# Transposes of the last attention step in the scores' banks, first gate_up weights split by halves, early splits issued behind the exponentials

## The chip, the core and the metric

The kernel runs on one core of a Trainium2 chip. The core has five engines with a queue each: TensorE (PE, matmuls and transposes; its weight loads are listed as PEld), VectorE (DVE), ScalarE (ACT), GpSimd (POOL) and SyncE (SP), which here only issues DMAs. The metric is the device time of one execution in microseconds. Before the change the median of 3 runs is 1319.53 us (1319.31 to 1319.69).

## The reference

One encoder block on x of 1024 rows by 1024 columns, in float32: a norm, a token mixer of a gated short convolution and an attention with 8 heads of 64, a merge of the two branches, an output projection, a second norm, a SwiGLU layer with 2816 hidden columns, and residual sums.

```python
h = rmsnorm(x, norm_mix_pre)
m = mixer(h, w_in, b_f, conv_w, w_branch, w_out)
x = x + rmsnorm(m, norm_mix_post)
h = rmsnorm(x, norm_ffn_pre)
f = swiglu(h, w_gate_up, w_down)
x = x + rmsnorm(f, norm_ffn_post)

# in the mixer
logits = q @ k.T * scale + c[q_pos] - c[k_pos]      # causal, per head
yb = softmax(logits) @ v
merged = sigmoid(gate_conv) * (ya @ w_branch[0]) + sigmoid(gate_attn) * (yb @ w_branch[1])
m = merged @ w_out
```

## The kernel before

**Products.** Each float32 operand is split into two parts of a shorter type: `split(hi, lo, src)` copies on ACT (`hi`) and subtracts on DVE (`lo = src - hi`), and a product of 128x128 by 128x512 is three matmuls. `lo` therefore always waits for `hi`. The large products (w_in, w_out, gate_up, down) are Strassen products of half-size blocks.

**Attention.** The heads are taken in pairs (j = 0 to 3) with the queries in blocks of 128 rows. A list `steps` of 24 steps says which blocks stand in a step: (7), (6), (5), (4), (3, 2), (1, 0) for the first three pairs. In step t of the loop at L1284 stand, in this order of the code: the scores of step t (`step_qk`, PE, into banks `sp` of the tag "S", two tiles of two banks each); the transposes of the probabilities of step t-1 (`turn_bank`, PE, into banks `tps` of the tag "T", two of them), each drained to `ptT` by ACT or DVE; the row maxima of step t (`row_max`: on DVE, `pt` and `nm`, which frees the score tile), and the exponentials (`expo`: on ACT, `pt`). The product with v (`pv_pair`, banks `po`) follows some steps behind. For a step with one block, the maxima and exponentials of head e = 0 come in the first half of the step (`now[0]`), those of e = 1 in the second (`now[1]`).

Between them `fills()` issues what is listed for the step: the ACT half of splits of later operands (`cuts`), whose DVE halves are collected in `lows` and issued at the end of the step, and from step 7 on twelve matmuls at a time of the convolution's branch product (`branch_a`, bank `pba`, closed by a DVE product into `um`). In steps 2 to 5 the splits are those of k and q of the second head pair (`hi<-lo`, `hi<-raw`), in step 6 those of two tiles of the convolution's output (`yh`, `yl`) and of one weight (`s4h`, `s4l`).

In this stage every engine keeps the order of the code (`strict[0] = engines`, L1107): an instruction that waits holds all that stands behind it on its engine.

After the last step (t = 24, `NU`) the ten transposes of step 23 remain, two `turn_bank` for each head, then the reciprocal of the row sums (`inverse(3)`, DVE), its transpose `tr` on PE (`inverse_rows`, in t = 25), and two small DMAs by way of DRAM that spread it over rows (`rb`), by which `yb` is divided before the second branch product (`pbb`).

**gate_up.** Its first four weights (`begin_early`, `f_begin`, `prep_first`) are begun while the w_out products and the second norm of the last row pairs still run (`e_norm`, `e_turn`). A weight is loaded into one of three buffers `raw` (512 KB), split, and its first half `LO` multiplied (A11), its second half `UP` later (A12). The same three buffers hold rows of the norm. Outside the attention a scheduler sets the order on each engine from the order of the code and from what it takes for each instruction's time, apart from calls that are `pinned`.

Of the kernel before, what the change touches and what calls it, by code (L numbers as in the profile page):

```python
# [10 lines left out]
F32 = mybir.dt.float32  # L11
# [6 lines left out]
P = 128  # L18
S = 1024
# [3 lines left out]
NC = 512  # L23
# [23 lines left out]
def block_kernel(  # L47
# [17 lines left out]
    engines = ("tensor", "vector", "scalar", "gpsimd", "sync")  # L65
# [28 lines left out]
    def pool(name, bufs=1, side="left", space=None):  # L94
        kw = dict(name=name, bufs=bufs)
        if space is not DRAM:
            kw["reuse_waits"] = "tile"
        if space is not None:
            kw["space"] = space
        else:  # L100
            kw["side"] = side
        stack = ExitStack()
        ctx.callback(stack.close)
        return stack.enter_context(tc.tile_pool(**kw)), stack.close

    def f32(ap):
        return ap.bitcast(F32)
# [4 lines left out]
    def sub(o, a, b):  # L112
        nc.vector.tensor_tensor(o, a, b, op=ALU.subtract)
# [14 lines left out]
    def copy(o, a):  # L128
        nc.scalar.activation(o, a, AF.Copy)

    def split(hi, lo, src):

        copy(hi, src)
        sub(lo, src, f32(hi))
# [9 lines left out]
    cpool, _ = pool("const")  # L144
    stat, _ = pool("stat", 4, side="right")
    stat.tile([P, 56], F32, name="pad", bufs=1)
    dpool, _ = pool("dram", space=DRAM)
# [383 lines left out]
    wpool, _ = pool("w")  # L531
# [4 lines left out]
    def kblk(t):  # L536
        return t.rearrange("p (a b) -> p a b", b=P)
# [4 lines left out]
    def raw_t():  # L542
        return wtile("raw", 3)

    def hi_t():
        return wtile("hi", 4, F32R)

    def lo_t():
        return wtile("lo", 3, F32R)
# [10 lines left out]
    def kmaj(src):  # L560
        return src.rearrange("(k p) m -> p k m", p=P)

    LO, UP = slice(0, 4), slice(4, 8)

    def prep_first(src1, there=None):

        if there is None:
            r1 = raw_t()
            nc.sync.dma_start(r1, kmaj(src1))
            h1, l1 = hi_t(), lo_t()  # L570
            split(h1, l1, r1)
        else:
            r1, h1, l1 = there
        return dict(A11=(h1[:, LO], l1[:, LO]), A12=(h1[:, UP], l1[:, UP])), r1
# [113 lines left out]
    def wcols(c0):  # L688
        return win[:, c0 : c0 + P]
# [147 lines left out]
    def p_cols(t, i, e):  # L837

        o = sum(x + 1 for x in steps[t][1] if x > i) * P
        return p_tile(t, e)[:, o : o + (i + 1) * P]  # L840
# [21 lines left out]
    def expo(t, i, e):  # L862

        c = e * ST + i
        pt = p_cols(t, i, e)
        nc.scalar.activation(
            pt, pt, AF.Exp, bias=nms.pop((t, i, e)), scale=-1.0,
            accum_out=rsums[steps[t][0]][:, c : c + 1],
        )

    def turn_bank(t, e, half, engine):

        n = sum(i + 1 for i in steps[t][1])
        ks = range(4 * half, min(4 * half + 4, n))
        if not ks:
            return
        if (t, e) not in ptTs:
            ptTs[t, e] = (
                t1.tile([P, ST, P], F32, tag="pT", name="ptT", bufs=6)
                if t  # L880
                else raw_t()
            )
        tps = pss.tile([P, 4, P], F32, tag="T", name="tps", bufs=2)
        for k in ks:
            nc.tensor.transpose(
                tps[:, k - ks[0], :], ps_[t, e][:, k * P : (k + 1) * P], ident
            )
        o, a = ptTs[t, e][:, ks[0] : ks[-1] + 1, :], tps[:, : len(ks), :]

        def drain():  # L890
            if engine == "ACT":
                copy(o, a)
            else:
                nc.vector.tensor_copy(o, a)

        return drain
# [3 lines left out]
    NU = len(steps)  # L900
# [95 lines left out]
    for ij, (kind, j, _, _) in enumerate(jobs):  # L996
# [10 lines left out]
        if ij < 2:  # L1007
            if ij == 0:
                r1 = raw_t()
                nc.sync.dma_start(r1, kmaj(wcols(jobs[1][2])))  # L1010
                t0_.tile([P, S], F32, tag="p", name="room", bufs=2)
                h1, l1 = (
                    kblk(t0_.tile([P, S], F32R, tag="cb", name=n, bufs=2)) for n in ("h1", "l1")
                )
# [8 lines left out]
            w = {**w, **prep_rest(wcols(jobs[ij][3]), r1)}  # L1023
            if ij == 1:
                pairs.q.append(pairs.prep(*pairs.srcs.popleft()))
            _, c12, c21, c22 = strassen(w, h1b, psm, pp, p1, mid)
# [7 lines left out]
        else:  # L1034
            w = pairs.get()
            psm_close()
            strict[0] = engines
            pss, pss_close = pool("pss", space=PSUM)
# [11 lines left out]
        elif kind == "gb":  # L1050
            for m, parts in ((j, (c11, c12)), (j + 1, (c21, c22))):
                zt = zts.pop(m)
                for n in range(2):
# [5 lines left out]
                    for t in (1, 0):  # L1059
                        back = 2 - t  # L1060
# [108 lines left out]
    def inverse(j):  # L1169

        invs[j] = st_tile("ri", 2 * ST)
        nc.vector.reciprocal(invs[j], rsums[j])

    def inverse_rows(j, psp, tag, bufs=1):

        tr = psp.tile([P, 4, P], F32, tag=tag, name="tr", bufs=bufs)[: 2 * ST, 0, :]
        nc.tensor.transpose(tr, invs[j], ident)

        def drain():
            rT = t0_.tile([H * ST, P], F32, tag="cT", name="rT")[: 2 * ST]  # L1180
            nc.vector.tensor_copy(rT, tr)
            for e in range(2):
                nc.sync.dma_start(
                    ri_dram[j][e].rearrange("(i p) -> i p", p=P), rT[e * ST : (e + 1) * ST, :]
                )
            rb = rbs[j] = tp_.tile([P, S], F32, tag="rb", name="rb", bufs=1)
            for e in range(2):
                nc.sync.dma_start(
                    rb[e * HD : (e + 1) * HD, :], ri_dram[j][e].partition_broadcast(HD)
                )  # L1190

        return drain
# [58 lines left out]
    cuts, at = defaultdict(list), defaultdict(list)  # L1251
# [32 lines left out]
    for t in range(2, NU + 2):  # L1284
        turned = None
        now = groups(t) if t < NU else ([], [])
        back = t - 1 if t <= NU else None
        wide = back and sum(i + 1 for i in steps[back][1]) > 6
        if t < NU:
            step_qk(t)  # L1290
        if t > 6:
            for u in due(t):
                pv_pair(u)
        if t in rows:
            turned = inverse_rows(rows[t], pst, "mb")
        if t == NU + 1:
            turned = inverse_rows(3, pss, "T", 2)
        lows, muls = [], []

        def fills():  # L1300
            lows.extend(f for f in (g() for g in cuts.pop(t, ())) if f)
            muls.extend(m for m in (next(fill, None) for _ in range(units.get(t, 0))) if m)

        if t == NU:
            fills()
        if back:
            da = turn_bank(back, 0, 0, "ACT")
            db = turn_bank(back, 0, 1, "DVE")
            da()
        if t <= 6:  # L1310
            for u in due(t):
                pv_pair(u)
        for i, e in now[0]:
            row_max(t, i, e)
        if t < NU and len(steps[t][1]) > 1:
            mask_of(t, steps[t][1][1])
        if turned:
            turned()
        if t == NU:
            for f in lows + muls:  # L1320
                f()
            lows, muls = [], []
        if back and db:
            db()
        for i, e in now[0]:
            expo(t, i, e)
        if t == NU:
            inverse(3)
        else:
            fills()  # L1330
        if back:
            dc = turn_bank(back, 1, 0, "ACT" if wide else "DVE")
            dd = turn_bank(back, 1, 1, "DVE" if wide else "ACT")
        for i, e in now[1]:
            row_max(t, i, e)
        if 7 < t < NU:
            for m in muls:
                m()
            muls.clear()
        if t == NU - 1:  # L1340
            for i, e in now[1]:
                expo(t, i, e)
        if back:
            dc()
            if dd:
                dd()
        if t < NU - 1:
            for i, e in now[1]:
                expo(t, i, e)
        if t + 1 < NU:  # L1350
            mask_of(t + 1, steps[t + 1][1][0])
        for f in lows + muls + at.pop(t, []):
            f()
# [152 lines left out]
    turned = []  # L1506
# [112 lines left out]
    for k in (0, 2):  # L1619
        w = ep.tile([P, D], F32, tag="t", name="wr", bufs=1)  # L1620
        cut_wo(w, ((B22, 4 + k, n2), (B22, 5 + k, n2)))

    def f_src(f):
        return wgu[:, f * P : (f + 1) * P], wgu[:, FH + f * P : FH + (f + 1) * P]
# [3 lines left out]

    def f_begin(n, b1, p1):
        f = FIRSTS[n]  # L1630
        w, _ = prep_first(f_src(f)[0])
        prod(b1, w["A11"], hb[B11], True)
        pinned(lambda: copy(p1, b1), *(("scalar",) if n >= 8 else ()))
        if f > 1:
            nc.gpsimd.dma_start(pre_dram[f][0], p1)
        begun[n] = w, b1, p1
# [90 lines left out]
    for n in range(4, NPRE + 1):  # L1727
# [6 lines left out]
        if n == 8:  # L1734
            for sl in range(4):
                a = slice(sl * P, (sl + 1) * P)
                b = slice(NC + sl * P, NC + (sl + 1) * P)
# [28 lines left out]
    for f in range(NF):  # L1766
        if f < NPRE:
# [7 lines left out]
            _, g2, u1_, u2 = strassen(rest.get(False), hb, psm, fp, p1, rest.more)  # L1775
# [275 lines left out]
```

## Time and profile before

| | us |
|---|---|
| median of 3 runs | 1319.53 |
| the profiled execution | 1319.29 |
| its span, from the first to the last instruction | 1317.2 |
| DVE busy in the span | 964.9 |
| ACT busy in the span | 556.8 |
| PE idle in the span (1317.2 - 1306.7) | 10.5 |

A row of a timeline gives the start in us from the span's start, the duration, the engine, the line (all have L76, that of the helper that records each call), the operation, what it writes and reads, the shape, and in brackets how long the engine was idle before it and what ended the wait. A row of waits gives who waited for whom: us in total, how often, the longest. PE's granted clock is 0.998 of full speed over the span.

A duration reaches past the point at which the next instruction can start: two ACT copies of 128x512, 0.6 us each by themselves, start 0.52 us apart.

### The profile page before, as it was taken

The page shows a single profiled execution, that of the slowest core. Times are in us where ns is not written, and L with a number is a line of the kernel's source. Part 1 is how long each engine was busy: PE and PEld are TensorE (multiplying, and loading weights), DVE is VectorE, ACT ScalarE, POOL GpSimd, SP SyncE. Part 2 cuts the span into 40 slices and gives each one's busy share as a digit, 9 for nine tenths or more (in the row PEclk, how much of TensorE's full clock was granted, in tenths as well). Part 3 has the DMA queues.
Part 4 walks back from the last instruction along what each step waited for, and adds up shares of the span by engine and source line. Part 5 has one row for each costly group of instructions (what it writes and reads, how often), then busy time and mean ns, then how long its engine had stood idle before and what let it go on. Part 6 is the DMA issues. An engine that isn't in the chain of part 4 may idle for free.

```text
span 1317.2 us, 17978 instructions
## 1 busy us (share of the span) xinstructions
PE 1306.7 (99%) x6710; PEld 1089.5 (83%) x6710; DVE 964.9 (73%) x1514; ACT 556.8 (42%) x895; POOL 142.4 (11%) x271
## 2 busy tenths in 40 slices
PE   9999999999999999999999999999999999999998
PEld 8988888888888888888888888888888888888886
DVE  6974878765656876686798788987766776676685
ACT  6642322243355866514577522322322234444452
POOL 0001000011012212020011021221001110000000
PEclk9999999999999999999999999999999999999999
DMA  6344544555536545465266455553223338866441
GB/s 217 113 120 136 150 123 121 153 164 146 152 120 200 161 144 171 152 232 208 76 228 207 153 168 177 176 184 104 97 88 118 106 111 282 317 249 193 158 168 64
DMA packets 189351, 211.00 MB, mean 160 GB/s; under 512 B 11584, under 2 KB 137600, under 8 KB 189264
## 3 DMA queue, kind: packets, MB, share of 16 engines
q1 hardware_dynamic: 155872, 146.64, 35.6%
q0 software_dynamic: 16496, 54.83, 11.2%
q10 hardware_dynamic: 16896, 8.39, 2.1%
q8 instruction: 52, 0.85, 0.3%
q14 instruction: 35, 0.29, 0.1%
HBM read 151.30 MB, written 58.52 MB: 159 GB/s over the span
## 4 chain that ended last, share of the span: by engine, by line
PE 96%; DVE 2%; ACT 1%; DMA 1%; issue 0%; SPq 0%; DVEq 0%; ACTq 0%
PE b L76 57%; PE pd L76 16%; PE pba L76 3%; PE pbb L76 3%; PE pv L76 3%; PE po L76 3%; PE tps L76 3%; PE p L76 2%; PE sp L76 2%; PE ma L76 1%; PE q L76 1%; PE tp L76 1%; PE mb L76 1%; DMA xt<-in_x_dram 1%; DVE t L76 0%
## 5 line engine op out<-in xcount | busy, mean ns | idle before, releaser
L76 PE MATMUL b<-x,hi 128*128 128x512 f32 x1088 | 335.3, 389 | 0.0
L76 PEld LDWEIGHTS b<-x,hi 128*128 128x128 f32 x1088 | 204.2, 188 | 42.1
L76 PE MATMUL b<-x,lo 128*128 128x512 f32 x544 | 211.7, 389 | 0.0
L76 DVE TENSOR_TENSOR c<-c,b 128x512 f32<-128x512 f32 x193 | 131.5, 681 | 62.2 <-PE b L76 54.7
L76 DVE TENSOR_TENSOR lo<-raw,hi 128x1024 fp32r<-128x1024 f32 x92 | 110.7, 1204 | 76.6 <-PE b L76 66.8
L76 ACT ACTIVATE hi<-raw 128x1024 fp32r<-128x1024 f32 (+1 forms) x99 | 100.6, 1018 | 97.3 <-PE b L76 49.8
L76 PEld LDWEIGHTS b<-x,lo 128*128 128x128 f32 x544 | 102.1, 188 | 21.2
L76 ACT ACTIVATE hi<-sx 128x1024 fp32r<-128x1024 f32 (+1 forms) x43 | 44.8, 1043 | 152.5 <-PE b L76 144.8
L76 ACT ACTIVATE sgf<-c 128x512 f32<-128x512 f32 x31 | 19.6, 633 | 131.9 <-DVE c L76 112.8
L76 DVE TENSOR_TENSOR lo<-sx,hi 128x1024 fp32r<-128x1024 f32 (+1 forms) x43 | 51.5, 1198 | 30.6 <-PE b L76 27.3
L76 DVE TENSOR_TENSOR sx<-raw 128x512 f32<-128x512 f32 x78 | 53.5, 687 | 14.4 <-DMA raw<-in_w_gate_up_dram 7.1
L76 PE MATMUL pd<-hi,lo 128*128 128x512 f32 x160 | 62.3, 389 | 0.0
L76 PE MATMUL pd<-hi 128*128 128x512 f32 x160 | 61.9, 390 | 0.0
L76 PE MATMUL pd<-ghi 128*128 128x512 f32 x148 | 57.6, 390 | 0.0
L76 PE MATMUL pd<-glo,ghi 128*128 128x512 f32 x148 | 57.6, 389 | 0.0
L76 PE MATMUL pd<-ghi,glo 128*128 128x512 f32 x148 | 57.6, 389 | 0.0
L76 PE MATMUL b<-hT34h,lo 128*128 128x512 f32 x136 | 52.9, 389 | 0.0
L76 PE MATMUL b<-hT34h,hi 128*128 128x512 f32 x136 | 52.9, 389 | 0.0
L76 PE MATMUL b<-hT34l,hi 128*128 128x512 f32 x136 | 52.9, 389 | 0.0
L76 PE MATMUL b<-hT12h,hi 128*128 128x512 f32 x136 | 52.9, 389 | 0.0
L76 PE MATMUL b<-hT12l,hi 128*128 128x512 f32 x136 | 52.9, 389 | 0.0
L76 PE MATMUL b<-hT12h,lo 128*128 128x512 f32 x136 | 52.9, 389 | 0.0
(425 smaller groups left out, 3015.4 us busy)
## 6 DMA issues: line engine op xcount, KB each, us to landing
raw<-in_w_gate_up_dram SPq DMA_DIRECT2D x55, 512.0 KB, 3.9
raw<-in_w_in_dram SPq DMA_DIRECT2D x35, 512.0 KB, 4.3
a_dramS<-um POOLq DMA_DIRECT2D x44, 256.0 KB, 3.0
a_dramA<-um POOLq DMA_DIRECT2D x33, 256.0 KB, 2.7
sg<-sg_dram SPq DMA_DIRECT2D x32, 256.0 KB, 3.9
x<-wo_dram SPq DMA_DIRECT2D x16, 512.0 KB, 5.8
graw<-a_dramS SPq DMA_DIRECT2D x14, 512.0 KB, 4.4
sg_dram<-c POOLq DMA_DIRECT2D x24, 256.0 KB, 3.4
```

The source lines that it names most:

```text
L76: ins = getattr(self.engine, name)(*args, **kw)
```

## The change

It has three parts.

1. In step 24 the reciprocal comes first; the ten transposes go into two tiles of the scores' tag "S" (`turn_bank` is given the tile), so that none of them waits for a drain; `tr` follows directly, and the drains, `fills()` and the rest come behind. `tr` is no longer in step 25.
2. `prep_first` can split by halves; for the first four weights of gate_up it does, in two copies and two subtractions of 128x512 in place of one each of 128x1024.
3. In steps 2 to 6 `fills()` stands behind the exponentials of the step's second half in place of ahead of that half. From step 7 on it stays where it was.

```diff
-    def prep_first(src1, there=None):
+    def prep_first(src1, there=None, halves=(slice(None),)):
...
-            split(h1, l1, r1)
+            for b in halves:
+                split(h1[:, b], l1[:, b], r1[:, b])
...
-    def turn_bank(t, e, half, engine):
+    def turn_bank(t, e, half, engine, at_=None):
...
-        tps = pss.tile([P, 4, P], F32, tag="T", name="tps", bufs=2)
+        if at_ is None:
+            tps = pss.tile([P, 4, P], F32, tag="T", name="tps", bufs=2)
+        else:
+            tps = at_[:, half].rearrange("p (a b) -> p a b", a=4)
...
-        if t == NU + 1:
-            turned = inverse_rows(3, pss, "T", 2)
...
         if t == NU:
+            inverse(3)
+            lasts = []
+            for e, engines in enumerate((("ACT", "DVE"), ("DVE", "ACT"))):
+                two = pss.tile([P, 2, NC], F32, tag="S", name="tps2", bufs=2)
+                lasts += [turn_bank(back, e, half, eng, two) for half, eng in enumerate(engines)]
+            turned = inverse_rows(3, pss, "T", 2)
+            for f in lasts[:2] + [turned] + lasts[2:]:
+                f()
             fills()
+            for f in muls + lows + at.pop(t, []):
+                f()
+            continue
...
-        if t == NU:
-            for f in lows + muls:
-                f()
-            lows, muls = [], []
...
         for i, e in now[0]:
             expo(t, i, e)
-        if t == NU:
-            inverse(3)
-        else:
+        if t > 6:
             fills()
...
         if t < NU - 1:
             for i, e in now[1]:
                 expo(t, i, e)
+        if t <= 6:
+            fills()
...
-        w, _ = prep_first(f_src(f)[0])
+        w, _ = prep_first(f_src(f)[0], halves=(LO, UP) if n < 4 else (slice(None),))
```

What the engines' queues hold, at three places.

ACT in step 3 (640 columns for each head), before and then with the change; `hi<-lo` is a half of the k split:

```order
L76 ACTIVATE ptT<-tps 128x512
L76 ACTIVATE pt,rsum<-pt,nm 128x640
L76 ACTIVATE hi<-lo 128x512
L76 ACTIVATE ptT<-tps 128x256
L76 ACTIVATE pt,rsum<-pt,nm 128x640
```

```order
L76 ACTIVATE ptT<-tps 128x512
L76 ACTIVATE pt,rsum<-pt,nm 128x640
L76 ACTIVATE ptT<-tps 128x256
L76 ACTIVATE pt,rsum<-pt,nm 128x640
L76 ACTIVATE hi<-lo 128x512
```

`hi` moved behind the second exponential. DVE at the end of step 3 and in step 4 (512 columns), which stands the same in both kernels:

```order
L76 COPY ptT<-tps 128x512
L76 TENSOR_TENSOR lo<-lo,hi 128x1024
L76 ISA pt,nm<-sp,cb 128x512
L76 ISA nm 128x1
L76 ISA pt,nm<-sp,cb 128x512
L76 ISA nm 128x1
```

The subtraction stands ahead of step 4's maxima as it did. DVE behind the divide of step 23, the difference (`tps_5480` and `tps_5487` are the two tiles of the scores' tag, one for each head):

```order
 L76 TENSOR_TENSOR yb<-yb,rb 128x512
-L76 TENSOR_TENSOR lo<-raw,hi 128x1024
+L76 RECIPROCAL ri<-rsum 128x16
+L76 COPY ptT<-tps_5480 128x128
+L76 COPY rT<-tr 16x128
+L76 COPY ptT<-tps_5487 128x512
 L76 TENSOR_TENSOR um<-sg,pba 128x512
-L76 COPY ptT<-tps 128x128
-L76 RECIPROCAL ri<-rsum 128x16
-L76 COPY ptT<-tps 128x512
+L76 TENSOR_TENSOR lo<-raw,hi 128x1024
```

The reciprocal has taken the place of `lo`. PE at the same place:

```order
 L76 MATMUL tps<-ident,pt 128x128 x6
+L76 MATMUL tps_5480<-ident,pt 128x128 x5
+L76 MATMUL tps_5487<-ident,pt 128x128 x5
+L76 MATMUL tr<-ident,ri 16x128
 L76 MATMUL pba<-yh_3761,s4h 128x512
```

The ten transposes and `tr` moved ahead of the twelve `pba` matmuls; before, the ten stood between `pba` and `po`, and `tr` behind `po`. ACT where gate_up begins, before and then with the change (`c`, `um`, `junk` and `sq` belong to the w_out products and the norm, `hi<-raw` to the gate_up weights):

```order
L76 ACTIVATE tt,ssq<-xt 128x1024
L76 ACTIVATE hi<-raw 128x1024
L76 ACTIVATE sq<-va 128x2
L76 ACTIVATE junk,qb<-keep 128x512
L76 ACTIVATE junk,qa<-p_6129 128x512
```

```order
L76 ACTIVATE tt,ssq<-xt 128x1024
L76 ACTIVATE hi<-raw 128x512 x3
L76 ACTIVATE sq<-va 128x2
L76 ACTIVATE hi<-raw 128x512
L76 ACTIVATE junk,qb<-keep 128x512
```

Of the four halves the third, which is of the fourth weight, stands ahead of the root `sq`, where the fourth weight's whole `hi` stood before. DVE a little earlier, with the change; before, one `lo<-raw,hi` of 128x1024 stood in the place of the first half, and none where the second stands:

```order
L76 SCALAR_TENSOR_TENSOR raw<-raw,r_6592,gpo 128x1024
L76 TENSOR_TENSOR lo<-raw,hi 128x512
L76 TENSOR_TENSOR c_6647<-c_6647,b_6622 128x512
L76 TENSOR_TENSOR xt<-xt,raw 128x1024
L76 SCALAR_TENSOR_TENSOR tt<-p_6096,r_6592,gpo 128x512
L76 SCALAR_TENSOR_TENSOR tt<-c_6508,r_6592,gpo 128x512
L76 TENSOR_TENSOR lo<-raw,hi 128x512
```

The second half of the second weight's `lo` has four operations ahead of it.

## Prediction

> **What bounds the kernel now.** I read the page's busy times first, then the list of what TensorE waited for, then the timelines of ScalarE (ACT) and VectorE (DVE) at the three edited places.
>
> ```profile
> PE 1306.7 (99%) x6710; PEld 1089.5 (83%) x6710; DVE 964.9 (73%) x1514; ACT 556.8 (42%) x895; POOL 142.4 (11%) x271
> PE tps L76 <- ACT ptT L76: 0.6, 1, 0.6
> PE tp L76 <- ACT um L76: 0.5, 1, 0.5
> ...
> PE tps L76 <- ACT pt L76: 0.2, 1, 0.2
> ```
>
> TensorE (PE) is busy for 1306.7 of 1317.2 us, and its matmuls are the same before and after. So the change can only give back waits of PE, or add some. The three waits shown are exactly the places that are edited: 0.58 us at the last transposes, 0.53 us where gate_up begins, 0.20 us in the early attention steps. Together 1.3 us is at stake on the good side, 0.1% of the time. The bad side has no such limit, so the question is whether a moved instruction makes PE wait for something new.
>
> **Early steps: the split behind the exponentials.** A split is two instructions: ACT writes `hi`, DVE then writes `lo` from it. The change moves only the ACT half; DVE's order there is unchanged, and in it `lo` stands ahead of the next step's score maxima (CUSTOM_DVE rows, ended by a READ_ACCUMULATOR row `nm`). The maxima free the score banks that PE's next scores wait for. The cover that hides this now is an idle ACT.
>
> ```profile
> 420.39 0.62 ACT L76 ACTIVATE hi<-lo 128x512 fp32r<-128x512 f32 x1
> ...
> 422.06 0.82 ACT L76 ACTIVATE pt<-pt,nm 128x640 f32<-128x640 f32 x1
> ...
> 429.06 0.60 ACT L76 ACTIVATE yb<-po 128x512 f32<-128x512 f32 x1 [0.91 <-PE po L76]
> ...
> 431.92 0.39 ACT L76 ACTIVATE pt<-pt,nm 128x128 f32<-128x128 f32 x1
> ...
> 433.12 1.15 ACT L76 ACTIVATE pt<-pt,nm 128x1024 f32<-128x1024 f32 x1 [0.19 <-DVE nm L76]
> ...
> 434.27 1.14 ACT L76 ACTIVATE yh<-raw 128x512 fp32r<-128x512 f32 x2
> 435.31 0.61 ACT L76 ACTIVATE s4h<-s 128x512 fp32r<-128x512 f32 x1
> ```
>
> ```profile
> 422.18 1.22 DVE L76 TENSOR_TENSOR lo<-lo,hi 128x1024 fp32r<-128x1024 f32 x1
> ...
> 425.68 0.08 DVE L76 DVE_READ_ACCUMULATOR2_ANT nm<- 128x1 f32 x1
> ...
> 431.19 0.69 DVE L76 SCALAR_TENSOR_TENSOR lo<-raw,hi 128x512 fp32r<-128x512 f32 x1 [0.67 <-ACT hi L76]
> 431.80 1.22 DVE L76 CUSTOM_DVE_ANT_0 pt<-sp,cb 128x1024 f32<-128x1024 f32 x1
> 432.94 0.08 DVE L76 DVE_READ_ACCUMULATOR2_ANT nm<- 128x1 f32 x1
> ...
> 436.88 1.08 DVE L76 CUSTOM_DVE_ANT_0 pt<-sp,cb 128x896 f32<-128x896 f32 x1
> ...
> 439.50 0.08 DVE L76 DVE_READ_ACCUMULATOR2_ANT nm<- 128x1 f32 x1
> ```
>
> ```profile
> 426.41 0.22 PE L76 MATMUL sp<-hi 64*128 64x128 f32 x2
> ...
> 432.08 0.33 PE L76 MATMUL tps<-ident,pt 128*128 128x128 f32 x1 [0.20 <-ACT pt L76]
> ...
> 440.01 0.44 PE L76 MATMUL sp<-hi 64*128 64x384 f32 x2
> ```
>
> Step 2 is harmless: its `hi` has no `lo` directly behind it. Step 3: `hi` now comes after the exponential of 422.06, so it starts at 422.06 + 0.82 = 422.88, ends 0.62 later at 423.50, and `lo` starts at 423.53 instead of 422.18: **1.35 us late**. All of DVE behind it shifts. The last `nm` of step 4 ends at 425.76 + 1.35 = 427.11 and PE's second score tile of step 5, which started at 426.41, starts at 427.17 (0.06 is what PE takes after a DVE end: below, `um` ends at 535.20 and `pba` starts at 535.26): PE is 0.76 late. Step 4 adds to DVE's lateness in the same way, but what decides next is step 5. There `yb` waits for PE, so at 429.06 + 0.76 = 429.82. The chain from `yb` to the end of the two 128-wide exponentials takes 432.30 - 429.06 = 3.24 (the last starts at 431.92 and holds ACT for its 0.39), of which 0.52 is the `hi` that leaves it (two such copies hold ACT for 1.04, 434.27 to 435.31). So `hi` starts at 432.54, ends at 433.16, and `lo` starts at 433.19 instead of 431.19: 2.00 late. The 0.20 us wait of 432.08 goes, but that lies inside this lateness.
>
> Step 6 is the worst: its three ACT copies stood between the two exponentials. The first `nm` ends at 433.02 + 2.00, so the exponentials run from 435.05, 1.15 each, and the copies start at 437.35 instead of 434.27. `yl`, `yl`, `s4l` follow 0.62 and 0.60 apart (437.97, 438.57, 439.17), and the maxima of step 7 start at 439.77 instead of 436.88: 2.89 late. Their second `nm` ends at 439.58 + 2.89 = 442.47, PE's second score tile of step 8 starts at 442.53 instead of 440.01. **Term 1: +2.5 us.** From step 7 on nothing is moved, and PE has hardly a wait left that could pay it back. Bounds: 1.7 (PE's 0.76 and the 0.9 that step 6 alone adds) and 3.0 (DVE's lateness in full).
>
> **The last transposes.**
>
> ```profile
> 534.32 0.82 PE L76 MATMUL tps<-ident,pt 128*128 128x128 f32 x6
> 535.26 0.50 PE L76 MATMUL pba<-yh,s4h 128*128 128x512 f32 x1
> ...
> 539.40 0.77 PE L76 MATMUL tps<-ident,pt 128*128 128x128 f32 x5 [0.58 <-ACT ptT L76]
> 540.10 2.62 PE L76 MATMUL po<-ptT,v 128*64 128x128 f32 x44
> 542.65 0.28 PE L76 MATMUL tr<-ident,ri 128*16 128x128 f32 x1
> ...
> 534.51 0.69 DVE L76 TENSOR_TENSOR um<-sg,pba 128x512 f32<-128x512 f32 x1 [1.61 <-PE pba L76]
> ...
> 536.92 1.22 DVE L76 TENSOR_TENSOR lo<-raw,hi 128x1024 fp32r<-128x1024 f32 x1
> ...
> 539.12 0.24 DVE L76 RECIPROCAL ri<-rsum 128x16 f32<-128x16 f32 x1
> ```
>
> The 0.58 us wait for a bank goes. But `tr`, which needs the reciprocal, now stands directly behind the ten transposes and ahead of `pba`. The reciprocal takes the place in DVE's queue where `lo` starts at 536.92, and ends at 537.16; `tr` can start at 537.22. Sixteen transposes from 534.32 at no more than 0.14 each (0.70 for five, 539.40 to 540.10) bring PE there by 536.56: it waits 0.7 us or more. Then come `pba` (2.86, from 535.26 to the transposes at 538.12), until 540.1, and `po` (2.55), until 542.66. Today PE stands at the same point at 542.68. **Term 2: 0.0**; bounds -0.7 (no wait for `tr`) and +0.2. The SP queue now sends four loads (gate tiles `sg` and parts of w_out) behind `rb` that went ahead of it. Who waits for the gate tiles is ACT and DVE, which empty eight banks there, and PE fills one in some 2.8 us; so I cost that at nothing, and at some tenths if that cover is gone.
>
> **gate_up by halves.**
>
> ```profile
> 669.71 1.07 ACT L76 ACTIVATE hi<-raw 128x1024 fp32r<-128x1024 f32 x1 [3.11 <-DMA raw<-in_w_gate_up_dram]
> ...
> 671.79 0.66 PE L76 MATMUL tp<-ident,tt 128*128 128x128 f32 x4 [0.53 <-ACT um L76]
> ...
> 674.35 0.74 DVE L76 SCALAR_TENSOR_TENSOR tt<-c,r,gpo 128x512 f32<-128x512 f32 x1
> 675.01 1.22 DVE L76 TENSOR_TENSOR x<-um,x 128x1024 fp32r<-128x1024 f32 x1
> ...
> 682.62 1.06 PE L76 MATMUL tp<-ident,raw 128*128 128x128 f32 x8
> ...
> DMA to landing us min/median/max: 3.6/5.5/5.8
> raw<-in_w_gate_up_dram SPq DMA_DIRECT2D x19, 512.0 KB, 4.8
> ```
>
> Eight more instructions at 0.1 us each hide on engines that are not the bound. The order costs more. Of the second weight's `lo`, the second half stands behind four DVE operations, which today end at 675.01; half of the first `lo` (0.54) is saved ahead of them, and a `va` that moved behind two normalisations costs some 0.5: so the half runs from about 675.0 to 675.65. Only then is its buffer free and the fourth weight's load issued, at 675.7 instead of behind the whole `lo` at 672.06. It lands 4.8 us later (the median of the window from 640 to 760 us), at 680.5. ACT has its first half *ahead of* the root `sq` of pair 2 (as it has the whole `hi` today, when the load is in time). From the landing: half `hi` 0.54, `sq` 0.21, DVE's reciprocal and a half `lo` 0.71, three small ones 0.58, the normalisation 1.27, to PE 0.06: 3.37, so PE's transposes of pair 2 start at 683.87. PE is there at 682.62 + 0.23 (one matmul now stands ahead of them): it waits 1.0. At a landing after 3.6 us it waits for nothing, at 5.8 for 2.0. **Term 3: +1.0**, bounds -0.5 (the 0.53 us wait gone, nothing late) and 2.0. The 0.53 us wait of 671.79 stays: `um` stands behind both halves, 0.1 later, and one matmul fills part of it.
>
> PE's 0.53 us wait for ACT is the row that a rule bears on. The Trainium skill, page Perfetto Trace Analysis, section Optimizing Scalar/DVE Operations, says that where these engines aren't saturated but cause bubbles on others, breaking up instructions may let work complete sooner. By that rule halves would take the 0.53 away; by the rows ACT stands idle for 3.11 us there for a load, and what PE needs is queued behind both halves.
>
> **The sum.** The profiled execution took 1319.29 us (span 1317.2 and 2.1 around it). +2.5 + 0.0 + 1.0 gives 1322.8; the median of the runs shown, 1319.53, is 0.24 higher, which the ranges include. 0.2%, about what a measurement of this kernel can tell from no change, is 2.64 us.
>
> **The rivals.**
> - *Only the early steps cost.* The fourth load runs nearly alone and lands within 3.9 us: term 3 is 0.1 and the time 1321.9, under 0.2%. For it: the minimum of 3.6. Against: stores of `xt` run beside it, and the median there is 4.8.
> - *Not slower: the score banks cover the late `lo`.* PE has two score tiles, and at step 8 it started 0.43 us after the `nm` it needs (439.58 to 440.01), at step 5 0.65. If DVE's lateness stays below that (because `hi` finds a hole in ACT ahead of the exponential, or DVE's maxima do not stand behind `lo`), PE sees none of it, the waits of 0.20 and 0.58 go, and the time is 1318.5. Against: the queues are in order, and 1.35 is twice 0.65.
> - *Halves help,* by the mechanism that PE's transposes of 671.79 come 0.53 sooner because ACT works in shorter pieces, and the load is not late: 1319.3 + 2.5 - 0.5 = 1321.3. The page of the skill named above speaks for it.
> - *The change doesn't do what it says* at the last transposes, since one wait is swapped for another: that is in term 2.
>
> **How the numbers follow.** Forecast 0.63, only the early steps 0.22, not slower 0.09, halves help 0.06. The forecast's own range is 1321.5 to 1324.5 (term 3 from 0.1 to 2.0, term 1 from 2.2 to 3.0), a small part of which (0.03) lies under 1322.2. So slower 0.60; within 0.2% takes that 0.03, the 0.22, the 0.06 and most of the 0.09: 0.37; faster 0.03, since even all three waits together are half of 2.64. The range reaches down to both smaller cases: 1320.9 to 1324.4.
>
> **What would show it.** Term 1: DVE idle for ACT `hi` for 1.3, 0.8 and 1.7 us and for `yh` for 1.4, PE idle for `nm` in the scores of steps 5 to 8. Term 2: the wait for `ptT` gone, one for `ri` of 0.7 to 1.1 us. Term 3: ACT idle for the fourth load, PE idle for DVE's normalised `raw` near 686 us. I am wrong if DVE shows no wait for `hi` in steps 3 to 5, or if PE catches up between steps 9 and 23.

## The result, and the profile after

The changed kernel takes 1323.03 us (median of 8 runs, 1321.97 to 1324.43) against 1319.60 us before (8 runs, 1319.31 to 1319.73): a ratio of 1.0026, 95% interval 1.0017 to 1.0035. That is slower: the whole interval lies above 1, though its lower end is under the 0.2% (2.64 us) that the prediction took as the least that can be told from no change. One run of the kernel before, beside the first experiments, took 4998.94 us and counts in no ratio. The profiled execution is the fastest of the eight: 1321.97 us, span 1320.1, that is 2.9 us over the span before.

First the page's busy times of the changed kernel, and the list of what PE waited for (total us, times, longest). Here and below only the rows that are read are shown, and rows between them are left out.

```profile
PE 1308.2 (99%) x6710; PEld 1089.6 (83%) x6710; DVE 964.1 (73%) x1518; ACT 557.0 (42%) x899; POOL 142.0 (11%) x271
PE tr L76 <- DVE ptT L76: 1.1, 1, 1.1
PE tps L76 <- DVE ptT L76: 0.6, 2, 0.3
PE sp L76 <- DVE nm L76: 0.4, 1, 0.4
PE p L76 <- ACT c L76: 0.2, 1, 0.2
```

All three waits that were edited are gone (0.58 for `ptT` from ACT, 0.53 for `um`, 0.20 for `pt`), and 2.3 us of others stand in their place. (The list also has 0.9 us for `hn`, 0.2 before, but at the very start: the transposes that waited begin at 7.38 us, before the change at 7.40.) PE's busy time is 1.5 us longer for the same 6710 matmuls. To see where along the kernel the time is lost, I take PE's rows at five places that both programs pass, from the timeline (start, us, engine, what, count). Before:

```profile
421.68 0.50 PE L76 MATMUL sp<-hi 64*128 64x512 f32 x2
445.40 3.50 PE L76 MATMUL po<-ptT,v 128*64 128x128 f32 x60
527.40 3.50 PE L76 MATMUL po<-ptT,v 128*64 128x128 f32 x60
542.68 0.47 PE L76 MATMUL pba<-yh,s4h 128*128 128x512 f32 x1
```

The fifth, 682.62, is in the prediction. After:

```profile
421.52 0.50 PE L76 MATMUL sp<-hi 64*128 64x512 f32 x2
448.01 3.50 PE L76 MATMUL po<-ptT,v 128*64 128x128 f32 x60
530.10 3.50 PE L76 MATMUL po<-ptT,v 128*64 128x128 f32 x60
545.52 0.50 PE L76 MATMUL pba<-yh,s4h 128*128 128x512 f32 x1
685.76 1.06 PE L76 MATMUL tp<-ident,raw 128*128 128x128 f32 x8
```

The changed kernel is 0.16 us *ahead* in step 3, which the change has not yet touched, and 2.61 behind at step 9: the early steps lose **2.77**. From there to the end of step 23 it loses 0.09, over the last transposes 0.14, and from there to the transposes of pair 2 in gate_up 0.30. Most of that 0.30 is no loss: one matmul more stands ahead of these transposes now, 0.23 us as the prediction counts it. At the next transposes of the norm both kernels have done the same matmuls again (before, then after):

```profile
697.33 1.07 PE L76 MATMUL tp<-ident,keep 128*128 128x128 f32 x8
700.23 1.07 PE L76 MATMUL tp<-ident,keep 128*128 128x128 f32 x8
```

The changed kernel is 2.90 behind there, 0.06 more than at 545.52, and that is the difference of the spans. So in this execution the early steps are nearly all of it.

**Early steps.** VectorE (DVE) and PE in the changed kernel, by the timeline; the bracket is the idle time before the row and what ended it.

```profile
428.73 0.69 DVE L76 SCALAR_TENSOR_TENSOR lo<-raw,hi 128x512 fp32r<-128x512 f32 x1 [1.16 <-ACT hi L76]
433.15 0.69 DVE L76 SCALAR_TENSOR_TENSOR lo<-raw,hi 128x512 fp32r<-128x512 f32 x1 [1.38 <-ACT hi L76]
438.02 1.29 DVE L76 TENSOR_TENSOR yl<-raw,yh 128x512 fp32r<-128x512 f32 x2 [1.42 <-ACT yh L76]
442.45 0.08 DVE L76 DVE_READ_ACCUMULATOR2_ANT nm<- 128x1 f32 x1
...
426.08 0.33 PE L76 MATMUL tps<-ident,pt 128*128 128x128 f32 x1 [0.32 <-DVE ptT L76]
430.64 0.55 PE L76 MATMUL tps<-ident,pt 128*128 128x128 f32 x3 [0.32 <-DVE ptT L76]
436.19 0.46 PE L76 MATMUL sp<-hi 64*128 64x448 f32 x1 [0.38 <-DVE nm L76]
```

DVE stands for ACT's `hi` (in step 6 `yh`) in steps 4, 5 and 6, where the profile before has a wait in step 5 alone (0.67), and the `nm` at the end of step 7 starts at 442.45. What PE shows for it is little: three waits of 0.3 to 0.4 us, 1.0 of the 2.77. The rest sits in rows that became longer, since several matmuls of one group are one row: the first scores of step 8, below, last 0.85 us where the row before the change had 0.44.

```profile
442.18 0.85 PE L76 MATMUL sp<-hi 64*128 64x384 f32 x2
```

**Last transposes.**

```profile
537.01 1.91 PE L76 MATMUL tps<-ident,pt 128*128 128x128 f32 x16
540.01 0.27 PE L76 MATMUL tr<-ident,ri 128*16 128x128 f32 x1 [1.09 <-DVE ptT L76]
539.98 0.09 PEld L76 LDWEIGHTS tr<-ident,ri 128*16 128x16 f32 x1 [1.30 <-ACT ptT L76]
...
539.62 0.24 DVE L76 RECIPROCAL ri<-rsum 128x16 f32<-128x16 f32 x1
```

PE waits 1.09 us at `tr`. The releaser that the trace names is a copy of `ptT`, but `tr` reads `ri`: the reciprocal ends at 539.86, the load of `ri` into PE starts 0.12 later and `tr` 0.15 later. The copy that is named ends at 540.01, when that load has begun, so it can't be what was waited for.

**gate_up.** ACT, SP's queue (the start of that row is the load's issue) and PE, as far as it is not above:

```profile
682.32 0.63 ACT L76 ACTIVATE hi<-raw 128x512 fp32r<-128x512 f32 x1 [0.43 <-DMA raw<-in_w_gate_up_dram]
...
678.38 0.37 SPq L76 DMA_DIRECT2D raw<-in_w_gate_up_dram  x1
...
674.38 0.49 PE L76 MATMUL p<-x,hi 128*128 128x512 f32 x1 [0.23 <-ACT c L76]
```

The fourth weight's load is issued at 678.38 and ACT has it 3.94 us later; PE's transposes at 685.76 have no wait. In the fastest of eight runs the late load just made it.

### The profile page after: what moved, and what is told of

The parts are those of the page before. It is cut to its first block, busy times and chain, and to the rows that moved or that the text cites. A ratio compares the mean times of both kernels' runs of the same rounds, so it can differ in the third digit from the quotient of the medians.

```text
span 1320.1 us, 17984 instructions
## 1 busy us (share of the span) xinstructions
PE 1308.2 (99%) x6710; PEld 1089.6 (83%) x6710; DVE 964.1 (73%) x1518; ACT 557.0 (42%) x899; POOL 142.0 (11%) x271
## 4 chain that ended last, share of the span: by engine, by line
PE 94%; DVE 2%; ACT 1%; DMA 1%; issue 1%; SPq 0%; DVEq 0%; ACTq 0%
PE b L76 57%; PE pd L76 16%; PE pba L76 3%; PE pbb L76 3%; PE pv L76 3%; PE p L76 2%; PE tps L76 2%; PE sp L76 2%; PE po L76 2%; PE ma L76 1%; PE q L76 1%; PE tp L76 1%; PE mb L76 1%; DMA xt<-in_x_dram 1%; DMA sx<-ya_dram 0%
## 5 line engine op out<-in xcount | busy, mean ns | idle before, releaser
L76 DVE TENSOR_TENSOR lo<-raw,hi 128x1024 fp32r<-128x1024 f32 (+1 forms) x96 | 111.4, 1160 | 76.4 <-PE b L76 66.5
```

What stands on the lines that cost most here:

```text
L76: ins = getattr(self.engine, name)(*args, **kw)
```

## The experiments

Each kernel was timed 6 to 11 times beside the kernel before on the same chip. Differences are those of the medians. The interval of a ratio is 2.4 us wide or more, so a difference below 1.2 us is not settled by the times alone; there the rows of the trace carry the argument.

**1. One part at a time.** Three kernels, each the kernel before with one part of the change; the diffs are those of the change.

> Only the early steps' splits go behind the second exponential; the last transposes and gate_up's weights stay as before. Theory (the split's DVE half comes late and stands ahead of the next step's maxima): 2.5 to 3.0 us over the kernel before, so about 1322.3, with runs that agree within 0.6 us, because nothing in these steps hangs on a transfer that varies. In its trace DVE is idle for ACT's hi in steps 3 to 5 and for yh in step 6, as in the changed kernel. Rival (the 2.5 us by which the changed kernel's runs differ among themselves come from the early steps): the runs of this kernel spread by 2 us too. Rival (the early steps are hidden by the score banks and another part costs): within 0.4 us of before.

Measured: 1322.29 us (1321.81 to 1322.83), 2.74 over before; ratio 1.0021 (1.0012 to 1.0030). PE in this kernel:

```profile
427.17 0.33 PE L76 MATMUL sp<-hi 64*128 64x128 f32 x2
448.15 3.50 PE L76 MATMUL po<-ptT,v 128*64 128x128 f32 x60
```

427.17 is the very time that the prediction worked out for step 5 (0.76 late), and 448.15 is 2.75 late, so the early steps hold this part's whole loss. (This execution, 1322.83, was the slowest of the eleven: it lost 0.57 more from step 9 to step 23, where no code differs from that before. The other traces lose 0.0 to 0.8 there against the profile before, so a difference of that size between two executions says nothing about an edit.) The expected spread of 0.6 was too tight: these runs spread by 1.0, and those of before, over 32 runs in this round, by 0.9.

> Only the last transposes go into the scores' banks, with the reciprocal ahead of step 24's split. Theory: one wait of PE is swapped for another (0.58 us for ptT against 0.7 to 1.1 for the transposed sums), so -0.1 to +0.4 us against before, median about 1319.7, spread under 0.6. Rival (loads that now stand behind rb in the SP queue make the gate tiles late): +0.5 us or more, with PE idle for banks that ACT and DVE have not emptied behind 545 us.

Measured: 1319.58 us (1319.01 to 1319.92), +0.03, ratio 1.0000 (0.9991 to 1.0009); the wait of `tr` is 1.09 us again. The swap is even. The runs spread by 0.9, over the expected 0.6, and PE shows no wait for the banks behind 545 us, so the rival of the late gate tiles falls.

> Only gate_up's first four weights are split by halves. Theory (the fourth weight's load is issued some 3 us later and lands after a time that varies from run to run): run by run between -0.2 and +2 us against before, median +0.5 to +1.0, and the runs spread by 1.5 us or more, as those of the changed kernel do. Rival (the halves cost nothing, the spread is from elsewhere): within 0.3 us of before and a spread under 0.6. Rival (halves help): -0.3 to -0.5 with a small spread.

Measured: 1319.82 us (1319.21 to 1320.87), +0.27, ratio 1.0002 (0.9993 to 1.0011). The median is below the expected 0.5 to 1.0, the spread of 1.7 is as expected. In its profiled execution the wait is there that the profile of the changed kernel did not show:

```profile
676.06 0.37 SPq L76 DMA_DIRECT2D raw<-in_w_gate_up_dram  x1
680.86 0.63 ACT L76 ACTIVATE hi<-raw 128x512 fp32r<-128x512 f32 x1 [1.22 <-DMA raw<-in_w_gate_up_dram]
684.30 1.06 PE L76 MATMUL tp<-ident,raw 128*128 128x128 f32 x8 [0.80 <-DVE raw L76]
```

4.80 us from issue to ACT's start, and PE waits 0.80.

**2. The early steps: DVE's queue, or ACT's order?**

> The move behind the second exponential for steps 2 to 4 alone; steps 5 and 6 keep their copies between the exponentials. Theory: DVE's lo of step 3 is 1.35 us late, PE's second score tile of step 5 is 0.76 late (as with all steps moved), and nothing behind adds to it: +0.8 us (0.5 to 1.1) against before, 1320.3. Rival (only steps 5 and 6 cost, the earlier lateness is made up by DVE's idle before step 6): within 0.3 us of before.

```diff
-        else:
+        elif not t in (2, 3, 4):
             fills()
...
+        if t in (2, 3, 4):
+            fills()
```

Measured: 1320.43 us (1320.13 to 1321.30), +0.92, ratio 1.0008 (0.9999 to 1.0017). PE's second score tile of step 5 in its trace, which is 0.24 ahead in step 3 (421.44 against 421.68):

```profile
426.94 0.33 PE L76 MATMUL sp<-hi 64*128 64x128 f32 x2
```

Against 426.41 before, and with the 0.24, that is 0.77 late. Here the `lo` of step 3, at 423.29, has its 1.27 us under ACT's `hi`.

> The same move for steps 2 to 4, and DVE's halves of these splits (lo) with the loads behind them are issued one step later, behind the score maxima of the next step. ACT's order and PE's work are as in the run for steps 2 to 4 alone. Theory (what costs is that the maxima stand behind a lo whose hi is late): the cost goes, within 0.3 us of before, and PE's second score tile of step 5 starts within 0.2 us of before's. Rival (it is ACT's new order that costs, the exponentials or the transposes' copies): +0.8 us as in the run for steps 2 to 4 alone.

```diff
         for i, e in now[1]:
             row_max(t, i, e)
...
+        for f in held:
+            f()
+        held = []
...
+        if t in (2, 3, 4):
+            held = lows + muls + at.pop(t, [])
+            continue
```

This stands on top of the move for steps 2 to 4. Measured: 1320.05 us (1319.60 to 1320.33), +0.54: between the two theories. The trace says why. PE:

```profile
426.37 0.22 PE L76 MATMUL sp<-hi 64*128 64x128 f32 x2
431.14 0.50 PE L76 MATMUL sp<-hi,lo 64*128 64x512 f32 x2 [0.59 <-DVE lo L76]
```

With the maxima in front of `lo`, PE's second score tile of step 5 is back at 426.37 (before: 426.41, and 0.76 late with all steps moved). So the 0.76 was the maxima's place behind `lo`, with ACT's order as in the run before. What this kernel loses is another thing, which my edit brought in: step 4's `lo` is now held until step 5, and step 6's scores read it, so PE waits 0.59 for it there. From step 3 to step 9 its trace loses 0.46, so that wait is most of the 0.54. For steps 5 and 6 the maxima were not put in front in any run; there the chain rests on the rows alone.

> The move for step 6 alone: its three copies go behind the second exponential. Theory (lateness adds up on DVE, and the two score tiles of PE absorb a part of it once): yl starts about 1.05 us later than before, PE has 0.43 us in hand at step 8, so +0.6 us (0.5 to 0.9). With steps 2 to 4 (0.8) that leaves some 1.3 of the 2.74 us to step 5. Rival (step 6's three copies are most of the cost, since they hold ACT longest): +1.5 us or more.

The diff is that for steps 2 to 4, with `t == 6`. Measured: 1320.29 us (1319.55 to 1321.03), +0.78; DVE in its trace:

```profile
435.92 1.29 DVE L76 TENSOR_TENSOR yl<-raw,yh 128x512 fp32r<-128x512 f32 x2 [0.90 <-ACT yh L76]
```

Before, `yl` started at 435.07 in a trace that is 0.14 later at this point (its `lo` of step 3 at 422.18 against 422.04 here): 0.99 late, where about 1.05 was worked out. Steps 2 to 4 (0.92) and step 6 (0.78) leave 1.04 of the 2.74 to step 5, by subtraction, since no run moved step 5 alone. The rows agree: from step 3 to step 9 these two traces lose 0.99 and 0.62 of the 2.77. So no step is the culprit; the lateness adds up in one queue.

**3. The last transposes: is the wait for the reciprocal needed?**

> The last transposes in the scores' banks, as in the change, but DVE's reciprocal of the last sums is issued at the end of step 23, ahead of the split and the division there, instead of behind them. Theory: the transposed sums' wait of 1.1 us on PE goes and the 0.58 us wait of before stays away: -0.5 us (-0.3 to -0.7) against before, about 1319.0. Rival (PE reaches its next wait sooner and stands there instead: a bank that ACT or DVE has not emptied, or the pv matmuls): within 0.2 us of before, and a new wait of about 0.5 us between 538 and 550 us.

Against the code of the change's last transposes:

```diff
         if t == NU:
-            inverse(3)
             lasts = []
...
+        if t == NU - 1:
+            inverse(3)
         for f in lows + muls + at.pop(t, []):
             f()
```

Measured: 1318.36 us (1317.90 to 1319.10), 1.15 *under* before, twice what was expected; ratio 0.9992 (0.9983 to 1.0000), so the interval just reaches 1. Each against the kernel before beside it, it is 4.6 us under the changed kernel. PE from step 23's probabilities to the `pba` that the two programs share, in this kernel:

```profile
527.92 3.50 PE L76 MATMUL po<-ptT,v 128*64 128x128 f32 x60
534.83 1.91 PE L76 MATMUL tps<-ident,pt 128*128 128x128 f32 x16
536.63 0.27 PE L76 MATMUL tr<-ident,ri 128*16 128x128 f32 x1
539.57 2.62 PE L76 MATMUL po<-ptT,v 128*64 128x128 f32 x44
542.13 0.50 PE L76 MATMUL pba<-yh,s4h 128*128 128x512 f32 x1
```

From 527.92 to 542.13 are 14.21 us; before, 15.28 (527.40 to 542.68), so 1.07 is won here. And `tr`, at 536.63, is ahead of the 128-wide copy of `ptT` (537.54 here), so it was indeed the reciprocal that it waited for in the changed kernel. 0.58 of the 1.07 is the wait for a bank. For the rest compare the transposes: sixteen in one row take 1.80 (534.83 to 536.63), while before, in groups of six, five and five, they took 0.94 (534.32 to 535.26), 1.28 (538.12 to 539.40) and 0.70 (539.40 to 540.10), 2.92 in all and 2.34 without the wait. That is 0.54, and little of it is the price of a group. In the kernel before:

```profile
450.30 0.82 PE L76 MATMUL tps<-ident,pt 128*128 128x128 f32 x6
538.12 0.71 PE L76 MATMUL tps<-ident,pt 128*128 128x128 f32 x5
```

Six transposes between `pba` and the scores take 0.75 there (450.30 to 451.05), three take 0.42 and eight 0.96: about 0.11 each, and 0.1 for the start of a group. The six of 534.32 took 0.19 more, because the `pba` behind them needs the bank that DVE's `um` reads until 535.20: it starts 0.06 after that, as the prediction says, and the chain of work that ended last runs through `um` there. No row shows this as a wait. The last 0.2 or so, by these rows, lie around the stop for the bank; what they are was not traced. So the change did win 0.58 + 0.54 here, most of it waiting by this estimate, and gave 1.09 back to the reciprocal behind the split and the division of step 23.

**4. gate_up: is it the late load?** The first try took the halves away from all but the first weight.

> Halves for gate_up's first weight alone; the second to the fourth are split whole, so the second weight's lo is one instruction again and stands ahead of the small operations of the next pair, and the fourth load can be issued as early as before. Theory: the spread of the runs falls below 0.6 us and the time is within 0.4 us of before. Rival (it is the halving itself, or PE's changed order behind it, that costs and varies, not the late issue of the fourth load): the same median and the same spread as with all four halved.

```diff
-        w, _ = prep_first(f_src(f)[0])
+        w, _ = prep_first(f_src(f)[0], halves=(LO, UP) if n < 1 else (slice(None),))
```

Measured: 1319.97 us (1319.49 to 1320.52), +0.42, spread 1.0, both over what was expected. The load is early again, but the scheduler made another order behind it: PE waits 0.65 for `um` and 0.15 for `raw`. It does not settle the question, and three kernels beside each other were run for it.

> The changed kernel itself once more, beside the next two. Theory (each part costs what it cost alone: 2.74, 0.03 and 0.27 us, and the last one varies with the landing of the fourth load): +3.0 to +3.5 us against before, spread of the runs over 1.5 us. In the profiled execution PE's wait for the normalised raw before the transposes near 685 us is 0 when the fourth load lands within 3.9 us of its issue, and about 0.9 us for each us that it lands later. Rival (the parts make each other worse): above +3.6.

Measured: 1323.26 us (6 runs, 1322.11 to 1324.39), 3.75 over before, ratio 1.0031 (1.0019 to 1.0043); by the median that is the rival (above 3.6), but the interval, 2.5 to 5.7 us, holds the theory's 3.0 to 3.5 and the first measurement's 3.43 as well. Its trace:

```profile
678.42 0.37 SPq L76 DMA_DIRECT2D raw<-in_w_gate_up_dram  x1
682.62 0.63 ACT L76 ACTIVATE hi<-raw 128x512 fp32r<-128x512 f32 x1 [0.65 <-DMA raw<-in_w_gate_up_dram]
686.06 1.07 PE L76 MATMUL tp<-ident,raw 128*128 128x128 f32 x8 [0.22 <-DVE raw L76]
```

Three executions now show the same chain at three landings: 3.94 us from issue to ACT and no wait of PE, 4.20 and 0.22, 4.80 and 0.80. So from about 4.0 us on PE seems to pay a us for a us: 0.58 more for a load that lands 0.60 later.

> The changed kernel, but DVE's half of the second weight's split is one instruction again (ACT's half stays in two pieces), so the fourth load is issued behind it some 3 us sooner. Theory: the fourth load is landed before ACT asks for it, no wait of ACT or PE for it is left, the median falls by 0.2 to 0.8 us against the changed kernel and the spread to about that of the kernel before (1 us). Rival (the varying time is not from this load): the same median and spread as the changed kernel beside it.

```diff
             for b in halves:
-                split(h1[:, b], l1[:, b], r1[:, b])
+                if whole:
+                    copy(h1[:, b], r1[:, b])
+                else:
+                    split(h1[:, b], l1[:, b], r1[:, b])
+            if whole:
+                sub(l1, r1, f32(h1))
...
+        w, _ = prep_first(..., whole=n == 1)
```

Measured: 1322.62 us (9 runs, 1322.11 to 1323.18), 0.64 under the changed kernel beside it, spread 1.1 against 2.3. Its trace (first SP's queue):

```profile
675.96 0.37 SPq L76 DMA_DIRECT2D raw<-in_w_gate_up_dram  x1
...
682.60 1.17 ACT L76 ACTIVATE hi<-raw 128x512 fp32r<-128x512 f32 x2
...
686.57 1.06 PE L76 MATMUL tp<-ident,raw 128*128 128x128 f32 x8
```

The load is issued 2.46 us sooner, and neither ACT's row nor PE's has a wait ahead of it. (The whole trace is later by 0.58 since the last `po`, 543.58 against 543.00, so PE's start can't be compared directly; from there to these transposes it takes 142.99 us here and 143.06 above.) The wait is therefore the late load's. In these two traces PE hardly gains by it: from the last `po` to the transposes of `keep`, where both have done the same matmuls, it takes 157.47 us here (to 701.05) and 157.53 above (to 700.53), since the wait for `c` grew from 0.28 to 0.45. That the spread of the times is too stays likely and not shown: the kernel before spread by 1.9 over its 26 runs in this round.

> The changed kernel without the halves in gate_up (early splits and last transposes as changed). Theory: 2.74 + 0.03, so +2.8 us (2.5 to 3.1) against before, with a spread of about 1 us, 0.3 to 0.7 us under the changed kernel beside it. Rival (the halves give something back once the other parts have shifted the work): the same as the changed kernel or above it.

Measured: 1322.23 us (1321.99 to 1323.50), +2.72, spread 1.5. The two parts without the halves cost what they cost alone (2.74 + 0.03). It is 1.03 under the changed kernel beside it, more than expected; by the medians the halves cost 0.7 to 1.0 us on top of the other parts (3.43 and 3.75 against 2.72), and 0.39 with the load in time, a difference that the times don't settle. The traces don't show this cost: from the last `po` to the transposes of `keep` this kernel takes 157.54 us and the changed one 157.26 and 157.53, since the wait for `um` that the halves remove is 0.82 here (0.53 before).

**5. The parts that help, together.**

> The splits of the early steps as before, the last transposes with the early reciprocal, and gate_up's first four weights in halves but for the second one's DVE half. Theory: -1.15 us from the transposes, as measured with these alone; the halves without the late load take PE's wait for um down from 0.5 us but leave a new one for c of 0.2 to 0.3: -1.0 to -1.5 us against before, about 1318.3. Rival (halves cost even without the late load, by the longer queues): -0.5 to -0.9.

Measured: 1318.41 us (1318.12 to 1319.07), -1.10, ratio 0.9992 (0.9983 to 1.0001), the same as with the transposes alone. The halves bring nothing even with the load in time: the wait for `um` (0.53) is now one for `c`, half a us too.

```profile
671.13 0.49 PE L76 MATMUL p<-x,hi 128*128 128x512 f32 x1 [0.48 <-ACT c L76]
```

## Why the prediction came out as it did

The forecast was 1322.8 us; the changed kernel took 1323.03 and, timed again, 1323.26, both inside the range. The mechanism was right for the early steps, which are most of the loss. That the sum came so close is in part luck: the forecast adds 3.5 us, the parts alone give 2.74 + 0.03 + 0.27 = 3.04, with the third at a quarter of its term, and the 0.4 from there to the measured 3.43 is not explained.

- **Early steps, predicted +2.5, measured 2.74** (part alone) and 2.77 (trace). Right in mechanism and place; the size was 0.25 small. DVE's idle times were expected as 1.3, 0.8, 1.7 for `hi` and 1.4 for `yh`; step 4's is 1.16, step 5's 1.38 and that for `yh` 1.42 (step 3's row, 1.27 us, names a transfer that ended together with `hi`). The `nm` of step 7 was to end at 442.47 and ended at 442.53, in an execution that was 0.16 ahead: 0.22 later than worked out, nearly all of the missing 0.25. 0.12 of it was there in step 5, where `yb` started 0.88 late (429.78) and not 0.76. I expected PE's idle time under `nm`; two of its three waits are under `ptT`, whose copies stand in the same queue of DVE. PE did not catch up behind step 9.
- **Last transposes, predicted 0.0, measured +0.03.** The wait for `ri` of 0.7 to 1.1 was 1.09, the upper end. The bound of 0.14 us for a transpose was wide: in one group they take 0.11, so PE came sooner and waited longer, and the reciprocal sets the end either way. What the prediction missed is how much there was to win: it took the waits that the profile lists, 0.58 here and 1.3 in all, for everything at stake, and with the reciprocal early this place alone gave 1.1.
- **gate_up by halves, predicted +1.0, measured +0.27 alone** and 0.7 to 1.0 with the other parts. The chain is as described: PE's wait was to begin at a landing of some 3.8 us and to be 1.0 at 4.8; it was 0 at 3.94 and 0.80 at 4.80. The median of 4.8 us that I took for the landing was the high end of what three executions showed from issue to ACT (3.9, 4.2, 4.8). The prediction kept the 0.53 us wait for `um`; it is gone, and PE stands one matmul earlier, for `c`. Why the same part costs more beside the other two is not settled: the intervals overlap, and the two profiled executions of the changed kernel, with waits of 0 and 0.22, don't show it. Executions that land later would, but none was profiled.
- **The rivals.** *The score banks cover the late `lo`* falls with the first run. *Only the early steps cost* holds for the profiled execution (a landing of 3.94 us, 1321.97) and not for the median. *Halves help*, by the rule of the Trainium skill named in the prediction (page Perfetto Trace Analysis, section Optimizing Scalar/DVE Operations), falls here: the wait for `um` did go (0.53 to 0), but a wait for `c` of 0.23 to 0.48 took its place, and in the version with everything in time nothing was left over. That one wait is swapped for another at the last transposes is so: 0.58 for 1.09.

## What to carry to other kernels

A two-engine operation is not moved by moving its first half: find where the second half stands in its own queue and who is queued behind it; here a `lo` that nobody read for two more steps delayed the maxima that PE needed next. A wait that disappears is only won if the next thing in line is ready, so look for the short instruction that now stands last (a 0.24 us reciprocal decided between +0.03 and -1.15 us). Splitting a load's consumer can delay the *next* load, whose buffer is free only when the last piece has been read.

## What was not expected of the hardware

A list of waits can miss much of what an engine waits for. In the early steps PE lost 2.77 us and shows 1.0 of it as waits; the rest is in rows of several matmuls that became longer (0.44 to 0.85 us for the first scores of step 8). At the last transposes 0.54 us went beyond the listed 0.58, 0.19 of it a wait for `um` that no row shows. And a named releaser can be wrong: `tr` waited for `ri`, and the trace names a copy of `ptT`.

The fourth load, 512 KB on the same queue at the same place of the program, reached ACT 3.9, 4.2 and 4.8 us after its issue in three executions of two kernels that issue it equally late.
